# Unused memory of 64 and 128 bytes between the pools of a one-core trunk layer, so that its operands start at other places modulo 256

## The chip, the cores and the metric

The kernel runs on one core of a Trainium2 chip. The metric is the device time of one execution in microseconds (us), the median of several runs. TensorE (PE in the profile) multiplies, with a weight load (PEld) ahead of every product; VectorE is DVE, ScalarE is ACT, GpSimd is POOL; SyncE (SP) starts most of the transfers. SBUF is the memory on the chip that the engines work in: 128 partitions, and in each of them a row of bytes. When this text says where a tile starts, it is the byte within the partition.

## The reference

One layer over 512 tokens of 1024 channels, all in float32:

```
u = rmsnorm(h); proj = u @ w_in                     # conv GLU | q | k | v | r | low rank | gates A, B
c = silu(layernorm(causal_dwconv31(a * sigmoid(g)))) ; y_conv = c @ w_conv_out
o = gated linear attention(q, k, v, decay), chunks of 64, 4 heads
y_gla = (rmsnorm(o) * silu(r)) @ w_gla_out
h = h + (sigmoid(gate_a) * y_conv + sigmoid(gate_b) * y_gla) @ w_o
z = causal_dwconv3(rmsnorm(h) @ w_up)               # 2 * 2816 channels
h = h + (silu(z_a) * z_b) @ w_down ; return rmsnorm(h)
```

## The kernel before

**Three products for one.** To get float32 results from the fast float32r products, every operand is split into a high part (rounded to float32r) and a low part (the rest). `whi` and `wlo` are the parts of a tile of weights, `uh` and `ul` those of the tokens; the other pairs (`ch` and `c`, `h`, `oa`, `xq`, `usq`, `gainq`, `btmpq`, `hq`, `sumsq`, `yh` and `yl`, `ah` and `al`, `sh` and `sl`) are the same for later activations. `mm3` then issues three products, which are lines 554 to 556 of the profile, and each of them has a weight load of its own:

```
nc.tensor.matmul(acc, ll, rh, start=first, stop=False, **kw)   # 554
nc.tensor.matmul(acc, lh, rl, start=False, stop=False, **kw)   # 555
nc.tensor.matmul(acc, lh, rh, start=False, stop=last, **kw)    # 556
```

The second argument is the operand that is loaded into the array (128x128, "loaded operand" below), the third is the one that streams through it (128x512 or 128x256, "streamed operand"). In `col_tile` the weights are loaded and the activations are streamed; in `seven` (Strassen-like products with seven parts for `w_r`, `w_o` and `w_down`) and in `row_half` the activations are loaded and the weights streamed; `two_tiles` streams activations of 256 columns.

**Order.** The program is one long list of products. The list `order` says in which order the tiles of weights are needed; SyncE loads each into a `raw` tile some steps ahead, ACT makes `whi`, DVE or an adding transfer of POOL makes `wlo`. Between these, DVE runs the 31-tap convolution (line 916), which is spread in small shares over the products of the first 250 us. In time the stages are: tokens and v (to about 33 us), GLU and low rank (to 113), v, heads of the attention with q and k (to 245), out-gate r (to 284), merge (to 424), `w_o` (to 464), then up- and down-projection of the channel mixer in three groups.

**Pools.** Tiles are taken from pools, which lie in SBUF one behind the other; a pool's tiles start at fixed places. From the left: constants (`cp`), weights (`wp`: `raw`, `whi`, `wlo`, 4 of each), tokens (`up`: `u`), temporaries (`tp`: first `x` and `gain`, then small tiles, then `tmp` and `btmp`), heap (`hp`: `h`), convolution (`vp`: `c`); later the pool `ffn` takes the place of the last two. From the right end of SBUF downward, behind `edge`: the attention's tiles, later `r`, `ch`, `late` (`sums`) and `hres`. Three pieces of unused memory, `PADS = (384, 992, 768)` bytes, lie in `cp`, `edge` and `tp`. With them `raw`, `whi`, `wlo`, `u`, `x`, `gain`, `h`, `c`, the pool `ffn` and everything on the right start at multiples of 256; `tmp` and `btmp` start at 128 modulo 256.

Of the kernel before, what the change touches and what calls it, by code (L numbers as in the profile page):

```python
# [10 lines left out]
F32 = mybir.dt.float32  # L11
# [7 lines left out]
P = 128  # L19
# [35 lines left out]
WARM = (6, 1)  # L55
MID = 4
EARLY = 2
PADS = (384, 992, 768)
ET = mybir.EngineType
SEVEN = {"w_o": KT // 2, "w_down": FT // 2, "w_r": KT // 2}  # L60

# [40 lines left out]
def trunk_layer(ctx: ExitStack, tc: tile.TileContext, a: dict, out: bass.AP):  # L102
    nc = tc.nc

    def pool(name, bufs, space=None):
        kw = {"space": space} if space is not None else {}
        return ctx.enter_context(tc.tile_pool(name=name, bufs=bufs, **kw))

    def scoped(name, bufs, side="left"):
        scope = ExitStack()  # L110
        return scope, scope.enter_context(tc.tile_pool(name=name, bufs=bufs, side=side))
# [3 lines left out]
    cp = pool("const", 1)  # L115
    wp = pool("weights", 1)
    up = pool("acts", 1)
    tp = pool("temps", 1)
    ps = pool("psum", 1, bass.MemoryType.PSUM)
    dram = pool("dram", 1, bass.MemoryType.DRAM)  # L120
    edge = ctx.enter_context(tc.tile_pool(name="edge", bufs=1, side="right"))
    heap_scope, hp = scoped("heap", 26)
    conv_scope, vp = scoped("conv", 10)
# [5 lines left out]
    def nm(s):  # L129
        return f"{s}_{next(names)}"  # L130
# [27 lines left out]
        return ps.tile([P, T], F32, tag="ax", name=nm("ax"), bufs=3)  # L158


    for i, part in enumerate((cp, edge)):
        part.tile([P, PADS[i] // 4], F32, name=nm("pad"))


    eps = cp.tile([P, 1], F32, name="eps")
# [11 lines left out]
    def load_consts():  # L177
        tc.keep_in_program_order(nc.sync.dma_start(pp, a["pp"]))
        nc.gpsimd.memset(shares.bitcast(F32), -1.0 / D)
        nc.gpsimd.memset(run64, 1.0)  # L180
        nc.gpsimd.memset(run64[:, 0:T:64], 0.0)

        kf = tmp(P)
        nc.gpsimd.memset(kf, 1.0)
        nc.gpsimd.affine_select(
            kf, kf, pattern=[[1, P]], compare_op=ALU.is_ge, fill=0.0, base=0, channel_multiplier=-1
        )
        nc.gpsimd.tensor_copy(keep, kf)
        nc.gpsimd.memset(att, 0.0)
# [659 lines left out]
    prefetch(LOOK)  # L849
    v_done(3, 0, acc)  # L850
    start.__exit__(None, None, None)
    tp.tile([P, PADS[2] // 4], F32, name=nm("pad"))
    load_consts()


# [462 lines left out]
    part = [None] * KT  # L1318
# [763 lines left out]
```

## Time and profile before

| | |
|---|---|
| median of 3 runs | 813.72 us (813.64 to 814.4) |
| the profiled execution | 813.83 us, of which 812.1 us are the span from the first to the last instruction |
| PE busy | 804.1 us, 99% of the span, 4176 products |
| PEld busy | 689.3 us, 85% |
| DVE, ACT, POOL busy | 707.0 (87%), 496.1 (61%), 188.5 (23%) us |
| transfers | 116.89 MB, 144 GB/s |

A product in the trace has a start and a modelled end, and products are pipelined, so that one of 0.39 us is followed by the next after some 0.23 us. What a product costs is therefore read from the distance between two starts, called its step below, and not from its own duration. In the timeline a row begins with the start and the duration in us.

### The profile page before, as it was taken

How to read it: one execution, taken by the hardware profiler on the slowest of the kernel's cores; microseconds unless marked ns; L12 is line 12 of the kernel's file. 1: busy time of each engine (PE TensorE's matmuls, PEld its weight loads, DVE VectorE, ACT ScalarE, POOL GpSimd, SP SyncE). 2: the span in 40 equal slices, each digit the busy share in tenths (PEclk: the TensorE clock that was granted, in tenths of full speed). 3: DMA queues.
4: the chain of work that ended last, by engine and by line, in shares of the span. 5: the costliest groups of instructions: out<-in, count | busy, mean ns of one | idle time of the engine just before them, and what ended most of it. 6: DMA issues, size and time to landing. Idle time of an engine off the chain costs nothing.

```text
span 812.1 us, 11427 instructions
## 1 busy us (share of the span) xinstructions
PE 804.1 (99%) x4176; PEld 689.3 (85%) x4176; DVE 707.0 (87%) x1120; ACT 496.1 (61%) x761; POOL 188.5 (23%) x166
## 2 busy tenths in 40 slices
PE   9999999999999999999999999999999999999997
PEld 7888888788888899989888898898889988899885
DVE  6779999998998898786778899979966999789896
ACT  6667788677647785593445655456445663356555
POOL 2025434332204222022011101320123310522010
PEclk9999999999999999999999999999999999999999
DMA  8488757755832533433458523145732446334662
GB/s 333 151 196 183 187 162 174 165 134 141 216 88 89 151 122 105 153 107 102 158 135 213 171 78 105 55 153 157 152 131 80 143 117 169 104 105 171 166 129 105
DMA packets 44217, 116.89 MB, mean 144 GB/s; under 512 B 10408, under 2 KB 16048, under 8 KB 44160
## 3 DMA queue, kind: packets, MB, share of 16 engines
q1 hardware_dynamic: 36800, 90.19, 32.5%
q0 software_dynamic: 7200, 25.69, 18.3%
q8 instruction: 33, 0.54, 0.3%
q10 hardware_dynamic: 160, 0.27, 0.1%
q14 instruction: 24, 0.20, 0.1%
HBM read 110.76 MB, written 3.74 MB: 141 GB/s over the span
## 4 chain that ended last, share of the span: by engine, by line
PE 77%; DVE 15%; issue 5%; ACT 2%; POOL 1%; DVEq 0%; ACTq 0%; POOLq 0%
PE mm L554 18%; PE mm L555 18%; PE mm L556 18%; DVE c L916 5%; PE cv L555 4%; PE cv L556 4%; PE cv L554 4%; DVE aside L916 3%; PE ax L555 2%; PE ax L556 2%; PE ax L554 2%; DVE wlo L437 1%; PE mm L772 1%; ACT whi L435 1%; DVE h L1605 1%
## 5 line engine op out<-in xcount | busy, mean ns | idle before, releaser
L554 PE MATMUL mm<-uh,wlo 128*128 128x512 f32 (+1 forms) x532 | 193.8, 364 | 0.1
L555 PE MATMUL mm<-ul,whi 128*128 128x512 f32 (+1 forms) x532 | 191.5, 360 | 0.0
L556 PE MATMUL mm<-uh,whi 128*128 128x512 f32 (+1 forms) x532 | 191.4, 360 | 0.0
L437 DVE TENSOR_TENSOR wlo<-raw,whi 128x1024 fp32r<-128x1024 f32 x82 | 95.7, 1174 | 29.0 <-ACT whi L435 24.9
L405 POOL TENSOR_TENSOR raw<-raw,raw 128x512 f32<-128x512 f32 x39 | 61.2, 1569 | 240.6 <-DVE wlo L437 133.0
L554 PEld LDWEIGHTS mm<-uh,wlo 128*128 128x128 f32 x532 | 100.5, 189 | 15.4 <-DVE wlo L477 0.5
L556 PEld LDWEIGHTS mm<-uh,whi 128*128 128x128 f32 x532 | 100.4, 189 | 15.4
L555 PEld LDWEIGHTS mm<-ul,whi 128*128 128x128 f32 x532 | 100.5, 189 | 14.7
L435 ACT CAST whi<-raw 128x1024 fp32r<-128x1024 f32 x82 | 79.0, 966 | 36.7 <-PE mm L556 16.3
L468 ACT CAST whi<-raw 128x1024 fp32r<-128x1024 f32 x80 | 83.5, 1047 | 29.1 <-PE mm L556 12.8
L477 DVE TENSOR_TENSOR wlo<-raw,whi 128x1024 fp32r<-128x1024 f32 x50 | 66.1, 1328 | 7.2 <-ACT whi L468 7.0
L435 ACT CAST whi<-kept 128x1024 fp32r<-128x1024 f32 (+1 forms) x40 | 40.1, 1008 | 31.2 <-DVE kept L381 15.7
L437 DVE TENSOR_TENSOR wlo<-kept,whi 128x1024 fp32r<-128x1024 f32 (+1 forms) x40 | 47.6, 1194 | 6.2 <-ACT whi L435 6.2
L916 DVE SCALAR_TENSOR_TENSOR c<-aside,btmp,c 128x247 f32<-128x247 f32 (+13 forms) x93 | 52.3, 568 | 0.0
L916 DVE SCALAR_TENSOR_TENSOR aside<-cv,pp,aside 128x255 f32<-128x255 f32 (+6 forms) x112 | 52.0, 464 | 0.0
L916 DVE SCALAR_TENSOR_TENSOR c<-cv,pp,c 128x247 f32<-128x247 f32 (+13 forms) x93 | 43.1, 464 | 2.3 <-ACT c L912 1.4
L470 ACT ACTIVATE wlo<-raw 128x1024 fp32r<-128x1024 f32 x28 | 29.4, 1058 | 18.9 <-PE mm L554 18.9
L1793 DVE SCALAR_TENSOR_TENSOR tmp<-mm,pp,tmp 128x511 f32<-128x511 f32 (+1 forms) x42 | 31.1, 742 | 3.6 <-ACT tmp L1790 3.5
L1408 ACT COPY tmp<-mm 128x256 f32<-128x256 f32 x38 | 14.1, 370 | 30.0 <-PE mm L556 29.6
L1793 DVE SCALAR_TENSOR_TENSOR tmp<-tmp,pp,tmp 128x511 f32<-128x511 f32 (+1 forms) x32 | 27.8, 888 | 0.4
L1564 DVE TENSOR_TENSOR hres<-hres,mm 128x512 f32<-128x512 f32 (+1 forms) x37 | 24.6, 674 | 2.2 <-PE mm L556 2.1
L555 PE MATMUL cv<-ul,whi 128*128 128x512 f32 (+1 forms) x72 | 25.6, 356 | 0.0
(518 smaller groups left out, 2084.8 us busy)
## 6 DMA issues: line engine op xcount, KB each, us to landing
raw<-in_w_up_dram SPq DMA_DIRECT2D x44, 512.0 KB, 3.6
raw<-in_w_glu_dram SPq DMA_DIRECT2D x16, 512.0 KB, 5.3
raw<-in_w_down_dram SPq DMA_DIRECT2D x16, 512.0 KB, 4.1
wlo<-in_w_glu_dram POOLq DMA_DIRECT2D x12, 512.0 KB, 7.1
kept<-in_w_down_dram POOLq DMA_DIRECT2D x9, 512.0 KB, 5.5
raw<-in_w_v_dram SPq DMA_DIRECT2D x8, 512.0 KB, 6.4
raw<-in_w_qk_dram SPq DMA_DIRECT2D x8, 512.0 KB, 6.2
raw<-in_w_gb_dram SPq DMA_DIRECT2D x8, 512.0 KB, 4.5
```

What stands on the lines that cost most here:

```text
L405: work = nc.gpsimd.tensor_tensor(out, x, y, ALU.add)
L435: nc.scalar.copy(hi, raw)
L437: two_low[:] = [nc.vector.tensor_tensor(lo, raw, hi.bitcast(F32), ALU.subtract)]
L468: nc.scalar.copy(hi, raw)
L470: pace[0] = nc.scalar.mul(lo, raw, -1.0)
L477: pace[0] = nc.vector.tensor_tensor(lo, raw, hi.bitcast(F32), ALU.subtract)
L554: nc.tensor.matmul(acc, ll, rh, start=first, stop=False, **kw)
L555: nc.tensor.matmul(acc, lh, rl, start=False, stop=False, **kw)
L556: nc.tensor.matmul(acc, lh, rh, start=False, stop=last, **kw)
L916: nc.vector.scalar_tensor_tensor(out[:, j:], x[:, : half_t - j], w, out[:, j:], ALU.mult, ALU.add)
L1564: done = nc.vector.tensor_tensor(hres[t, n][:, c], hres[t, n][:, c], acc[:, c], op)
L1793: nc.vector.scalar_tensor_tensor(z[:, s:], acc[:, : T - s], w[j], z[:, s:], ALU.mult, ALU.add)
```

## The change

Three more pieces of unused memory: 64 bytes at the end of `wp`, 64 bytes at the end of `up`, 128 bytes in `vp`; and the piece in `edge` grows by 64 bytes. Nothing else is edited: the same instructions stand in the same order on every engine, with the same waits, and each tile has the same place among its pool's. What moves is where the tiles start. From the allocations of the two programs, the first byte modulo 256:

| tiles | before | after |
|---|---|---|
| `raw`, `whi`, `wlo` (`wp`) | 0 | 0 |
| `u`: `uh`, `ul` (`up`) | 0 | 64 |
| `x`, `gain`, with `kept`, `xq`, `gainq`, `oa` in their places (`tp`) | 0 | 128 |
| `tmp`, `btmp` with `btmpq` (`tp`) | 128 | 0 |
| `h`, `hq` (`hp`) | 0 | 128 |
| `c` (`vp`) | 0 | 0 |
| `ffn`: `kept`, `y`, `f`, `w`, `v`, `yh`, `yl`, `ah`, `al`, `sh`, `sl`, `usq` | 0 | 128 |
| the right side: attention, `r`, `ch`, `sums` with `sumsq`, `hres` | 0 | 192 |
| constants, with `shares` (96) and `ident` (32) | as they are | the same |

The 3929 float32r products of lines 554 to 556 and 772 have 2670 times 512 and 1259 times 256 columns. Of the streamed operand of one and the loaded operand of the next (the two that are read at the same time), the places modulo 256 differ before in 2 products of 512 columns and 65 of 256; after, in 2584 and 1156.

```
-PADS = (384, 992, 768)
+PADS = (384, 1056, 768)
+SHIFTS = (64, 64, 128)
...
-    for i, part in enumerate((cp, edge)):
-        part.tile([P, PADS[i] // 4], F32, name=nm("pad"))
+    for part, size in ((cp, PADS[0]), (edge, PADS[1]), (vp, SHIFTS[2])):
+        part.tile([P, size // 4], F32, name=nm("pad"), bufs=1)
...
-    tp.tile([P, PADS[2] // 4], F32, name=nm("pad"))
+    for part, size in ((tp, PADS[2]), (wp, SHIFTS[0]), (up, SHIFTS[1])):
+        part.tile([P, size // 4], F32, name=nm("pad"), bufs=1)
```

## The prediction

> **What bounds the kernel now.** I read the busy times first, then the waits of TensorE, then the stretches, then single starts in the timeline.
>
> ```profile
> span 812.1 us, 11427 instructions
> PE 804.1 (99%) x4176; PEld 689.3 (85%) x4176; DVE 707.0 (87%) x1120; ACT 496.1 (61%) x761; POOL 188.5 (23%) x166
> PEclk9999999999999999999999999999999999999999
> ...
> PE mm L675 <- DVE ones L647: 1.1, 1, 1.1
> PE cv L554 <- DVE r L1621: 0.3, 1, 0.3
> ...
> PEld ax L1251 <- DVE state L1240: 1.1, 3, 0.5
> PEld mm L555 <- DVE wlo L437: 0.7, 2, 0.5
> ```
>
> TensorE is busy all the time at the full granted clock, and the last four rows, among the longest waits of the products and of their weight loads for another engine, add up to 3 us. So the span is the sum of the steps of 4176 products, and only what changes a step, or makes TensorE wait where it does not now, changes the time. The steps of two quiet stretches (first and last rows of runs of products of one kind):
>
> ```profile
> 341.99 0.28 PE L555 MATMUL cv<-sumsq,whi 128*128 128x256 f32 x1
> ...
> 342.95 0.40 PE L554 MATMUL mm<-oa,wlo 128*128 128x512 f32 x1
> 343.19 0.40 PE L555 MATMUL mm<-oa,whi 128*128 128x512 f32 x1
> 343.42 0.39 PE L556 MATMUL mm<-oa,whi 128*128 128x512 f32 x1
> ...
> 344.11 0.39 PE L556 MATMUL mm<-oa,whi 128*128 128x512 f32 x1
> ...
> 791.70 0.39 PE L555 MATMUL mm<-wlo,sh 128*128 128x512 f32 x1
> ...
> 800.31 0.39 PE L554 MATMUL mm<-whi,al 128*128 128x512 f32 x1
> ```
>
> Eight products of 256 columns take 0.96 us, 120.0 ns each; 38 of 512 columns take 8.61 us, 226.6 ns each. The difference, 106.6 ns, pays for 256 columns; so 512 columns cost 213.2 ns, and in both cases 13.4 ns are left over that do not depend on the columns. That remainder comes once for each product and its weight load, and it is the only thing of TensorE's that the change can touch: 13.4 ns x 3929 float32r products are 52.6 us, 6.5% of the span. In between, after the switch from 256 to 512 columns at 342.95, five products take 1.16 us, 232 ns each, before the steps fall back to 226.6: the remainder is not a constant of the array, it depends on what stood before.
>
> **What of it hangs on the place.** In these stretches all operands start at 0 modulo 256. Two kinds of products do not. In the first, `btmpq` is streamed from 128 between `usq` and weights at 0:
>
> ```profile
> 532.89 0.28 PE L554 MATMUL cv<-btmpq,wlo 128*128 128x256 f32 x1
> 533.00 0.28 PE L555 MATMUL cv<-usq,whi 128*128 128x256 f32 x1
> 533.12 0.28 PE L556 MATMUL cv<-btmpq,whi 128*128 128x256 f32 x1
> ...
> 534.30 0.28 PE L554 MATMUL ax<-gainq,wlo 128*128 128x256 f32 x1
> 534.41 0.28 PE L555 MATMUL ax<-xq,whi 128*128 128x256 f32 x1
> ```
>
> Twelve products take 1.41 us, 117.5 ns each, where 12 at 0 take 1.44. With both rows rounded to 0.01 us this is 2.5 ns less, give or take 0.8; I take 2. The first two show steps of 0.11 and 0.12 us, the one at 534.30 again 0.11. So the place does move the step, and here downward. In the second, `sum` is streamed from 128, against `shares` at 96 and then weights at 0, in two products of 512 columns:
>
> ```profile
> 306.65 0.39 PE L556 MATMUL mm<-h,whi 128*128 128x512 f32 x1
> 306.88 0.63 PE L1028 MATMUL ax<-sum,shares 128*128 128x512 f32 x2
> 307.34 0.28 PE L554 MATMUL mm<-uh,wlo 128*128 128x256 f32 x1
> ...
> 331.26 0.62 PE L1028 MATMUL ax<-sum,shares 128*128 128x512 f32 x2
> 331.72 0.39 PE L554 MATMUL mm<-oa,wlo 128*128 128x512 f32 x1
> ```
>
> Both pairs take 0.46 us, 230 ns each: 3.4 ns more than the quiet 226.6, though 2 to 4 ns less than the 232 to 234 at which the first products after a switch from 256 columns run (0.47 us for the two from 342.95), which the second pair is. One row says faster, one row says either; neither shows a long run with a constant distance, and that is what the change makes.
>
> **The change part by part.** Nothing is added, removed or moved in time on any engine or queue: no instruction, no wait, no transfer. Four kinds of users see other places.
>
> Products. 1156 of 256 columns now have the streamed and the next loaded operand apart, 65 had before: 1091 more. At the -2 ns of the `btmpq` row this is -2.2 us. Of 512 columns 2584 are apart, 2 before. Their price is bounded by -11.4 ns below (the remainder shrinks to 2, see the rivals) and by +5.4 above (every step is 232, as after a switch). I take -2 ns, since the remainder was the same 13.4 ns for both widths and so belongs to the weight load and not to the columns, and the `btmpq` row, the only one with more than two products in a row, prices such a load: -5.2 us.
>
> The elementwise engines. They read the tiles at other places too, and these rows say that it costs nothing (`tmp` and `btmp` start at 128, `f`, `ah` and `raw` at 0):
>
> ```profile
> L1807 DVE TENSOR_TENSOR f<-tmp,tmp 128x512 f32<-128x512 f32 x11 | 7.5, 683 | 0.2
> L1813 DVE TENSOR_TENSOR al<-f,ah 128x512 fp32r<-128x512 f32 x11 | 7.5, 683 | 0.4 <-ACT ah L1812 0.4
> L435 ACT CAST whi<-raw 128x512 fp32r<-128x512 f32 x16 | 9.9, 620 | 0.6 <-POOL raw L405 0.6
> L1066 ACT CAST ch<-btmp 128x512 fp32r<-128x512 f32 x8 | 4.7, 616 | 0.1
> ```
>
> DVE's 683 ns from 128 and from 0 are equal, ACT's 616 and 620 nearly; I put 0 for both.
>
> The transfers. `raw` and `wlo`, most of the bytes, stay at 0; `x`, `gain`, `kept`, `hres`, `rx` and the stored `y` go from 0 to 128 or 192, `tmp` from 128 to 0. The one pair of rows of equal size:
>
> ```profile
> out_dram<-tmp SPq DMA_DIRECT2D x2, 256.0 KB, 2.2
> out_dram<-hres SPq DMA_DIRECT2D x2, 256.0 KB, 2.1
> ```
>
> From 128 it took 0.1 us longer than from 0. The loads are covered by TensorE, which waits for none of them above; uncovered are the first `x` at the start and the last store at the end, so +0.1 to +0.2 us, which is rounding.
>
> The cover. A shorter step is worth its length only where the weights are ready, and that is DVE's and ACT's matter:
>
> ```profile
> 100.00:180.00 80.00, 79.87 (x361) 65.89 (x360) 79.87 (x172) 63.13 (x105) 30.54 (x28) 1.00 0.64 155
> 180.00:245.00 65.00, 64.97 (x297) 54.10 (x297) 61.91 (x136) 39.46 (x76) 10.97 (x11) 1.00 0.64 155
> 530.00:680.00 150.00, 150.00 (x841) 131.53 (x840) 128.21 (x169) 79.88 (x111) 33.66 (x26) 1.00 0.46 130
> ```
>
> (The columns are PE, PEld, DVE, ACT, POOL busy with counts.) From 100 to 180 us DVE, with the convolution, has 0.13 us of idle time; 361 products x 2 ns = 0.7 us would be gained there, and 0.6 of it is lost to waiting for DVE. From 180 to 245 DVE has 3.1 us free against 0.6, from 530 to 680 21.8 against 1.7: nothing is lost.
>
> Sum: -2.2 - 5.2 + 0.6 = -6.8 us. The profiled execution took 813.83 us (span 812.1 and 1.7 around it), 0.1 above the median of 813.72. 813.8 - 6.8 = 807.0 us.
>
> **A rule against it.** The Trainium skill, "TensorE: Matmul & The Clock Gate", section "Step-by-step: what each phase is for", says that TensorE reads the streamed operand and the weights through two independent ports, so that loading the next weights takes no bandwidth from the running product; "SBUF — State Buffer", section "Who interferes with whom", says that TensorE and ScalarE never wait on anyone. By these the place could not matter and the time would stay at 813.8. The trace disagrees in part: its remainder is 13.4 ns, and 117.5 ns stand against 120.0 with nothing else changed.
>
> **The rivals.**
>
> *The two reads stop hindering each other (much faster).* If the remainder is mostly two streams that meet at the same place modulo 256 all the time, a constant distance ends it. What is then left shows in the plain float32 products, which run each product in two records:
>
> ```profile
> 183.88 0.59 PE L1253 MATMUL ax<-state,q 128*128 128x256 f32 x2
> 184.31 0.59 PE L1251 MATMUL ax<-h,att 128*128 128x256 f32 x2
> ```
>
> 0.43 us for two records, 215 ns each, about as long as 512 columns (213.2): a remainder of 2. Then 11.4 ns x (1091 + 2584) = 41.9 us go, less 4.0 of the 4.1 us from 100 to 180 and 0.3 of 3.4 from 180 to 245, where DVE holds: about 776; half of that gives 794. Against it: the `btmpq` products had a distance of 128, and their steps do not fall to 109. Chance 0.15.
>
> *No distance matters, only a break in the run (no change).* In the `btmpq` rows the place alternates from product to product, 128, 0, 128. It may be the alternation that shortens steps, while any constant distance settles at 226.6 and 120.0 again. After the change the streamed operand starts at the same place as the one before it in about 9 of 10 products, so little is left: a tenth of 7.4 us, within 0.2% (1.6 us, about what a measurement of this kernel tells from no change). 813.1. The rule above gives the same. Chance 0.15.
>
> *The quiet step is the good case (slower).* 226.6 is near the low end of the steps of 512 columns seen (the 230 and 232 above), 120.0 the high end of those of 256. Where the distance keeps the two reads from settling, the wide products go to 230 to 232 and the narrow ones to 118: 2584 x 3.4 to 5.4 ns = +8.8 to +14.0, less 2.2: 820 to 825.5, with nothing to hide it, as TensorE is the bound everywhere. It decides as soon as a wide product loses 0.85 ns, for that eats the 2.2 us. For it: the pairs at line 1028. Against it: the second pair is quicker than the products that otherwise stand there. Chance 0.28.
>
> **How the numbers follow.** The forecast (a remainder smaller by 1 to 5 ns) has the other 0.42: 807.0, from 811.6, if the narrow products alone gain, to 798, if the wide ones gain twice what I took. With the much faster case, faster by over 0.2% is 0.57; same 0.15; slower 0.28. The range reaches into both outer cases: down to 790, past half of the large gain, which leaves out about 0.10, and up to 824, which leaves out the upper end of the slow case, about 0.06.
>
> **What would show it.** The starts in the timeline, in a long run of one kind: streamed tokens at 64 against weights at 0 (up-projection, from 500 us), loaded `sh`, `ah`, `yh` at 128 against streamed weights at 0 (the last 60 us). 224 to 225 and 117 to 119 ns there bear out the forecast, 226.6 and 120.0 the rival of no change, 228 and more the slow one, 216 the large gain. The durations at lines 435, 1807 and 1813 should stay at 620 and 683, the store of `tmp` and `hres` at 2.1 to 2.2 us. The sum is wrong if the steps differ with the distance, 64, 128 and 192 not being alike (I have a row for 128 alone), or if from 100 to 245 us DVE becomes what TensorE waits for although the steps got shorter.

## The result, and the profile after

The change made the kernel slower: 820.52 us, median of 4 runs (819.18 to 821.69), against 813.88 for the kernel before beside it. The ratio is 1.0081, with a 95% interval from 1.0069 to 1.0094. In a later series of 5 runs it was 820.03 us, ratio 1.0073 [1.0059, 1.0087]. The forecast was 807.0 and faster; the time lies inside the range and is that of the rival "the quiet step is the good case".

The busy times of the profiled execution (821.69 us):

```profile
span 819.9 us, 11427 instructions
PE 812.4 (99%) x4176; PEld 688.5 (84%) x4176; DVE 708.1 (86%) x1120; ACT 496.5 (61%) x761; POOL 190.1 (23%) x166
PEclk9999999999999999999999999999999999999999
```

The span grew by 7.8 us, PE's busy time by 8.3, and nothing else grew by more than 1.6. The clock is the same. The waits of products and weight loads for another engine:

```profile
PE mm L676 <- DVE ones L648: 1.1, 1, 1.1
PE cv L555 <- DVE r L1623: 0.2, 1, 0.2
...
PEld ax L1253 <- DVE state L1242: 0.5, 2, 0.2
...
PEld mm L556 <- DVE wlo L438: 0.3, 1, 0.3
```

They are no longer than before. So the 7.8 us are in the steps. These are the starts at the places of the program that the prediction quoted (lines 554 to 556 of before are 555 to 557 here):

```profile
39.64 0.40 PE L557 MATMUL mm<-uh,whi 128*128 128x512 f32 x1
...
74.88 0.40 PE L555 MATMUL mm<-uh,wlo 128*128 128x512 f32 x1
...
344.73 0.28 PE L555 MATMUL cv<-sumsq,wlo 128*128 128x256 f32 x1
...
346.11 0.40 PE L555 MATMUL mm<-oa,wlo 128*128 128x512 f32 x1
...
348.91 0.28 PE L555 MATMUL mm<-uh,wlo 128*128 128x256 f32 x1
...
499.83 0.39 PE L557 MATMUL cv<-uh,whi 128*128 128x512 f32 x1
...
519.98 0.39 PE L555 MATMUL mm<-uh,wlo 128*128 128x512 f32 x1
...
798.82 0.40 PE L555 MATMUL mm<-whi,sl 128*128 128x512 f32 x1
...
809.79 0.39 PE L557 MATMUL mm<-whi,ah 128*128 128x512 f32 x1
```

- Tokens at 64 against weights at 0, wide: 151 steps from 39.64 take 35.24 us, 233.4 ns each. The same kind of product from 499.83: 88 steps in 20.15 us, 229.0 ns. The same distance gives two values; more on that below.
- `sumsq` at 192, narrow: 12 steps in 1.38 us, 115 ns, 120.0 before.
- `oa` at 128, wide: 12 steps in 2.80 us, 233.3 ns. Before, these fell back to 226.6 after five products; now they don't.
- Loaded `sh`, `yh`, `ah` at 128, streamed weights at 0: 47 steps in 10.97 us, 233.4 ns; 226.6 before.

All starts of both traces, summed: the 512-column products took 620.3 us before and 630.8 after, those of 256 columns 167.6 and 165.0. That is +10.5 and -2.6, together +7.9, which is the growth of the span. The 3929 products that the prediction priced have +10.2 and -1.9 of this; the 32 and 80 products on other lines have +0.3 and -0.8, with what they wait.

The stretch with `btmpq`, where `usq` now starts at 128 and `btmpq` at 0, so that the place still alternates:

```profile
537.92 0.28 PE L555 MATMUL cv<-btmpq,wlo 128*128 128x256 f32 x1
...
539.33 0.28 PE L555 MATMUL ax<-gainq,wlo 128*128 128x256 f32 x1
```

Twelve products in 1.41 us, exactly as before. The elementwise groups, the stores and the three stretches:

```profile
L436 ACT CAST whi<-raw 128x512 fp32r<-128x512 f32 x16 | 9.9, 620 | 0.5 <-POOL raw L406 0.4
L1809 DVE TENSOR_TENSOR f<-tmp,tmp 128x512 f32<-128x512 f32 x11 | 7.5, 682 | 0.2
L1815 DVE TENSOR_TENSOR al<-f,ah 128x512 fp32r<-128x512 f32 x11 | 7.5, 681 | 0.3 <-ACT ah L1814 0.3
L1068 ACT CAST ch<-btmp 128x512 fp32r<-128x512 f32 x8 | 4.7, 616 | 0.1
```

```profile
out_dram<-tmp SPq DMA_DIRECT2D x2, 256.0 KB, 2.6
out_dram<-hres SPq DMA_DIRECT2D x2, 256.0 KB, 2.5
```

```profile
100.00:180.00 80.00, 80.00 (x360) 65.70 (x359) 78.81 (x170) 64.47 (x107) 30.53 (x27) 1.00 0.64 156
180.00:245.00 65.00, 65.00 (x296) 54.12 (x295) 61.90 (x138) 40.24 (x77) 11.11 (x12) 1.00 0.64 152
530.00:680.00 150.00, 150.00 (x843) 130.48 (x842) 125.88 (x168) 78.98 (x111) 33.51 (x25) 1.00 0.47 132
```

682 and 681 against 683, 620 and 616 as before: the elementwise engines don't notice. From 100 to 180 us DVE now has 1.2 us of idle time where it had 0.13, as longer products on TensorE would give it.

### The profile page after: what moved, and what is told of

Its sections match the earlier page's. It is cut to its first block, busy times and chain, and to the rows that moved or that the text cites. A ratio compares the mean times of both kernels' runs of the same rounds, so it can differ in the third digit from the quotient of the medians.

```text
span 819.9 us, 11427 instructions
## 1 busy us (share of the span) xinstructions
PE 812.4 (99%) x4176; PEld 688.5 (84%) x4176; DVE 708.1 (86%) x1120; ACT 496.5 (61%) x761; POOL 190.1 (23%) x166
## 4 chain that ended last, share of the span: by engine, by line
PE 97%; DVE 1%; ACT 1%; issue 0%; DVEq 0%; ACTq 0%
PE mm L555 23%; PE mm L556 23%; PE mm L557 23%; PE cv L555 4%; PE cv L557 4%; PE cv L556 4%; PE ax L555 3%; PE ax L556 3%; PE ax L557 3%; PE mm L773 2%; PE ax L1253 1%; PE cv L773 1%; PE ax L1255 1%; PE ax L1235 1%; PE ax L684 1%; PE mm L780 0%
## 5 line engine op out<-in xcount | busy, mean ns | idle before, releaser
L555 PE MATMUL cv<-uh,wlo 128*128 128x512 f32 (+1 forms) x72 | 25.6, 355 | 0.0
```

## The experiments

Theory A in the texts below says that a product's step hangs on the distance, modulo 256, between the place of its streamed operand and that of the next loaded one. The other theories are told in the texts themselves, and what became of each stands behind its text. "Distance" below is streamed minus loaded.

### The steps by themselves

A separate kernel without the layer: 50 sections of 36 float32r products each, nothing beside them, so that nothing but the places and the columns differs from section to section. It leaves out the whole layer and computes only these products.

```
def section(n, count, cols, streams, loads):
    for i in range(count):
        m = streams[i % len(streams)] // 4 + T * (i % 4)   # first word of the streamed operand
        w = loads[i % len(loads)] // 4 + P * (i % 8)       # of the loaded one
        nc.tensor.matmul(acc, loaded[:, w : w + P], streamed[:, m : m + cols], ...)
```

> Not the layer: 50 sections of 36 float32r products each, with nothing beside them, so that only the steps of TensorE are measured. The loaded and the streamed operand start at chosen places modulo 256. Theory A (the distance of the two operands sets the step, whatever else the core does): the sections at distance 0 run at 226.7 ns (512 columns) and 120.0 ns (256), whether both operands stand at 0 or both at 64, 128 or 192; the sections at 64, 128 and 192 run at 229 to 234 ns and 116 to 119 ns, as in the changed layer. Theory B (a start that is no multiple of 256 is what costs): both at 64 runs as slowly as 64 against 0, above 229 ns. Theory C (the step comes from what ACT, DVE and transfers do at the same time): here all sections are alike, at one step for each width.

The timeline of single sections ("wide" has 512 columns, "narrow" 256; wide at distance 0, 32, 64, 128 and 192; narrow at 0, 64 and 192; wide with both operands at 64; wide at 4; and three sections with alternating places, told below). A row puts together 32 to 35 products: the start, then the time from the first start to the last end.

```profile
19.50 7.87 PE L109 MATMUL bank<-streamed,loaded 128*128 128x512 f32 x34
36.01 8.09 PE L109 MATMUL bank<-streamed,loaded 128*128 128x512 f32 x34
52.80 7.95 PE L109 MATMUL bank<-streamed,loaded 128*128 128x512 f32 x34
86.09 8.06 PE L109 MATMUL bank<-streamed,loaded 128*128 128x512 f32 x34
119.68 8.09 PE L109 MATMUL bank<-streamed,loaded 128*128 128x512 f32 x34
161.27 4.12 PE L109 MATMUL bank<-streamed,loaded 128*128 128x256 f32 x33
178.32 4.05 PE L109 MATMUL bank<-streamed,loaded 128*128 128x256 f32 x33
212.34 3.90 PE L109 MATMUL bank<-streamed,loaded 128*128 128x256 f32 x33
229.19 7.89 PE L109 MATMUL bank<-streamed,loaded 128*128 128x512 f32 x34
278.81 8.20 PE L109 MATMUL bank<-streamed,loaded 128*128 128x512 f32 x34
295.48 8.21 PE L109 MATMUL bank<-streamed,loaded 128*128 128x512 f32 x35
303.75 8.15 PE L109 MATMUL bank<-streamed,loaded 128*128 128x512 f32 x35
312.09 3.90 PE L109 MATMUL bank<-streamed,loaded 128*128 128x256 f32 x32
```

Of 7.87 us, 0.39 are the last product's own; the other 7.48 are 33 steps of 226.7 ns. In the same way 8.09 gives 233, 7.95 gives 229, 8.06 gives 232, 8.20 gives 237. The settled steps, as means of the last 24 of each section:

| distance | 0 | 16 | 32 | 48 | 64 | 80 | 96 | 112 | 128 | 144 | 160 | 176 | 192 | 208 | 224 | 240 |
|---|---|---|---|---|---|---|---|---|---|---|---|---|---|---|---|---|
| wide, ns | 226.7 | 231.7 | 233.3 | 233.3 | 228.9 | 231.1 | 233.3 | 231.1 | 232.1 | 233.3 | 234.4 | 233.3 | 233.3 | 234.7 | 233.3 | 226.7 |
| narrow, ns | 120.0 | 118.6 | 116.7 | 118.3 | 117.8 | 120.0 | 120.0 | 113.3 | 118.8 | 118.7 | 117.3 | 119.4 | 113.3 | 119.2 | 118.3 | 117.1 |

At 4 bytes a wide product takes 236.7 ns, the most of all, at 8 bytes 233.3. Both operands at 64, at 128 or at 192 give 226.67, as at 0. Only the loaded one at 64 gives 233.3, as the streamed one at 192 does; only the loaded one at 192 gives 228.9, as the streamed one at 64 does. So it is the difference that counts, and nothing but these products is needed for it: no other engine is at work here, and no transfer of operands. At distance 0 the two widths go opposite ways: of 16 distances, it is the best for wide products, together with 240, and the worst for narrow ones, together with 80 and 96. B and C fall.

Theory A holds as long as the places stay the same from product to product. Four sections let both places alternate between 0 and 128. Where each streamed operand has the place of the next loaded one (distance 0 throughout, as theory A counts it), the steps are 230.0 ns wide (the row at 295.48) and 116.7 narrow (312.09), and not 226.7 and 120.0. Where it has the place of its own product's loaded operand, so that the next one lies 128 away, they are 228.3 (303.75) and 116.7, and not 232.1 and 118.8. So the distance to the next loaded operand does not set the step alone. Whether its own loaded operand counts as well, or the change of place itself, these sections leave open; at constant places the two loaded operands stand alike.

### Everything at 64

The kernel before, with all operands of the products moved together by 64 bytes, so that every distance stays what it was.

```
-PADS = (384, 992, 768)
+PADS = (448, 928, 768)
```

> The kernel before with 64 bytes more in the first piece and 64 less in the one at the right edge: all tiles that stood at 0 modulo 256 stand at 64, tmp and btmp at 192, and the distances are those of before. Theory A (distance): steps of 226.7 and 120.0 ns and 813 to 815 us. Theory B (multiples of 256): steps of 230 to 233 and 118 ns in most products and 819 to 822 us, as with the change.

813.87 us against 813.89, ratio 0.9998 [0.9988, 1.0007]. The sums are 620.4 us for 512 columns and 167.6 for 256, as before. That is theory A's forecast (813 to 815 us) and not B's (819 to 822): in the layer, too, a common step of 64 bytes costs nothing.

### The tokens alone

Of the change, only the step of `u` to 64 is made (the piece in `up` brings the pools behind it back to their places).

```
-SHIFTS = (64, 64, 128)
+SHIFTS = (64, 192, 0)
```

> One part of the change alone: the tokens' pool at 64, everything else at the places of before. 1320 wide and 612 narrow products stream tokens or later sums from there against weights at 0, 312 wide ones load them. Theory A: the products that touch the pool run as after the change (230.4 and 118.1 ns streamed, 233.3 loaded), all others at 226.7 and 120.0: 1320 x 3.7 + 312 x 6.6 - 612 x 1.9 ns = +5.8 us, 819 to 820.5 us. If what costs is instead that places alternate between pools (a rival, since the change made four places of one), the tokens alone, all at one place in long runs, cost under 2 us: 813.5 to 816 us.

815.20 us, ratio 1.0019 [1.0009, 1.0029]: a small loss where a large one was expected. The long run of wide tokens:

```profile
39.66 0.39 PE L555 MATMUL mm<-uh,wlo 128*128 128x512 f32 x1
...
74.91 0.39 PE L556 MATMUL mm<-ul,whi 128*128 128x512 f32 x1
```

154 steps in 35.25 us: 228.9 ns, the value of the separate kernel for 64, and not the 233.4 of the changed layer. The 512-column sum is 624.6 us (+4.3), the 256-column sum 164.8 (-2.8): the 583 narrow products with tokens at 64 took 116.8 ns on average, and the 300 wide ones that load from this pool at 64 took 233.3, as their distance of 192 says. Theory A's forecast was missed: it priced the streamed tokens by the changed layer, at +3.7 ns wide and -1.9 narrow, where they moved by +1.9 and -3.3. The time lies in the band of the rival, but not for its reason: products at a constant distance did become dearer, from 226.9 to 233.3 ns where the pool is loaded.

### Entry, width and type

A second separate kernel, again without the layer, of 69 sections in three parts. The first runs a section at distance 64 behind sections of other kinds. The second replaces one operand by a single word that is read again and again, or both by bf16. The third puts runs of 12 or 24 narrow products between runs of 12 or 24 wide ones at 0; here it is the loaded operand's place that is set to 64, 144 and 224, which makes the distances 192, 112 and 32.

```
x, y = s[:, m : m + cols], l[:, w : w + P]
if kind == "one word streamed":
    x = s[:, m : m + 1].to_broadcast([P, cols])
if kind == "one word loaded":
    y = l[:, w : w + 1].to_broadcast([P, P])
nc.tensor.matmul(acc, y, x, ...)
```

> Not the layer: sections of products alone, as in e1. Three questions. (1) In the changed layer the long run of the tokens' products at distance 64 goes 233, 233, 234 ns, with the tokens alone moved it goes 226, 229, 232: same operands, same distance. Theory A1 (a distance has more than one cycle to settle in, and what stood before decides): the sections at 64, entered from wide ones at 0, 128 and 32 and from narrow ones, settle on at least two different means. Theory A2 (something else in the layer): all settle at 228.9, as in e1. (2) Theory A (two reads at a time): with one word streamed again and again, or one word loaded, the remainder over 213.3 ns falls well below 13 and the distance no longer matters; if the remainder belongs to the weight swap alone, it stays at 13.4 ns. With bf16 operands, half the bytes, the remainder falls too, to a few ns. (3) Runs of 12 narrow at distance 0, 64, 144, 224 between 12 wide at 0: with 64 or 144 as the place of the streamed operand I expect no better than e1's single runs, 118 ns in the mean.

Rows of single sections: narrow at 0 behind wide at 64; narrow at 64 behind wide at 64; one word streamed, wide; bf16, wide; bf16, narrow.

```profile
51.71 4.12 PE L118 MATMUL bank<-streamed,loaded 128*128 128x256 f32 x33
...
64.26 3.90 PE L118 MATMUL bank<-streamed,loaded 128*128 128x256 f32 x33
...
129.97 7.50 PE L118 MATMUL bank<-streamed,loaded 128*128 128x512 f32 x34
...
170.31 7.50 PE L118 MATMUL bank<-half,turned 128*128 128x512 bf16 x34
...
201.40 3.77 PE L118 MATMUL bank<-half,turned 128*128 128x256 bf16 x33
```

- Entry. Wide products at 64 settled at 228.9 behind each of five predecessors (wide at 0, 32 and 128, narrow at 0 and at 64); 233.3 was not reached in this way, as theory A2 says. Narrow products at 64 did show two cycles: 113.3 ns here (3.90 us less 0.28 for the last, over 32 steps), 117.8 in the first kernel, where narrow ones stood before, and 117.8 again in a run of five in this kernel, which stood behind wide ones at 64 as the 113.3 did. So the kind of product that stood before does not decide alone.
- Type. In bf16 a wide product takes 215.83 ns and a narrow one 109.17, at 0, 64, 128 and 192 alike. Their difference, 106.66 ns, is the price of 256 columns; 2.5 ns remain. This is the 215.7 ns that the Trainium skill ("TensorE: Matmul & The Clock Gate", "Wait — 56ns, not 53.3ns?") gives for 512 columns, 512/2.4 + 2.5: for bf16 the rows agree with it, for float32r they show 226.67 to 236.7.
- Which read. With one word streamed, float32r falls to 215.83 ns at distance 0 and 64, and to 111.67 for narrow products at 0. With one word loaded, wide products do not fall, against the expectation: they take 231.1 ns at distance 0 (226.7 with the whole operand) and 231.7 at 64 (228.9). Narrow ones at 0 fall from 120.0 to 113.3. For wide products, what lies above 2.5 ns therefore needs the float32r stream through many addresses; the loaded operand need not come from many. How the two reads hinder each other no run shows, and no section leaves the weight load out.
- Short runs. Twelve narrow products took 119.4 ns each at distance 0, 117.75 at 192, 118.7 at 112, 116.5 at 32. The 113.3 of long runs at 112 and 192 is not reached. Nor is it in runs of 24, which hold 117.8 at 192 from the first step on and 119.3 at 112, so the length alone is not what keeps them from it. Twelve wide ones behind a switch took 228.8 to 229.8 on average, with steps such as 233 236 228 233 231 226 before they settled.

### Narrow products at 192, and at 32

The first kernel's table asks for another arrangement: wide products stay at distance 0, and only the weights that meet the 256-column tokens move. The `whi` and `wlo` slots get 64 more words, and the weights of `two` start 16 words into them, which makes the distance 192; with 56 words it is 32.

```
+ROOM, APART = 64, 16        # the second kernel: 64, 56
-                hi = wp.tile([P, D], F32R, tag="whi", name=nm("whi"), bufs=4)[:, :n]
+                at = APART if name == "two" else 0
+                hi = wp.tile([P, D + ROOM], F32R, tag="whi", name=nm("whi"), bufs=4)[:, at : at + n]
...
-PADS = (384, 992, 768)
+PADS = (128, 224, 0)
```

> The kernel before (all places at 0), with the weights of the 256-column units alone moved: their whi and wlo begin 64 bytes into the slot, so that the streamed operand lies 192 above the loaded one. Each of the eight slots is 256 bytes larger, and the unused pieces shrink to (128, 224, 0). Theory A: e1 gives 113.3 ns at distance 192 against 120.0 at 0; some 1190 narrow products gain up to 6.7 ns, -8 us, of which runs of 12 to 24 between wide ones keep half to all: 806 to 810 us, wide products unchanged at 226.7. If no gain survives in short runs (rival): 812 to 814.

> As the kernel with the narrow products' loaded weights 64 bytes further, but 224 bytes further, so that streamed minus loaded is 32 modulo 256. Theory A, with the steps measured in runs of 12 between wide products (116.5 at 32 against 117.8 at 192 and 119.4 at 0, and wide products behind them 0.7 ns dearer): narrow sum down by about 2.9 x 1100 = 3.2 us, wide sum up by up to 0.7 x 300 = 0.2: 810.7 to 811.2, against 812.1 at 192. Rival (short runs never reach their settled cycle in the layer, so all distances of narrow products but 0 give about the same): 811.9 to 812.5.

| | time, us | ratio to before | 512 columns, us | 256 columns, us |
|---|---|---|---|---|
| before | 813.94 and 813.97 beside the two | | 620.3 | 167.6 |
| narrow at 192 | 812.07 (811.63 to 812.82) | 0.9979 [0.997, 0.9988] | 620.5 | 165.4 |
| narrow at 32 | 812.00 (811.4 to 813.09) | 0.9976 [0.9967, 0.9985] | 620.9 | 165.1 |

Both beat the kernel before, and so the changed one too, by a small margin. The size that theory A gave from long runs was missed. In the kernel at 192:

```profile
284.67 0.28 PE L557 MATMUL mm<-ul,whi 128*128 128x256 f32 x1
...
285.24 0.28 PE L556 MATMUL mm<-uh,wlo 128*128 128x256 f32 x1
...
339.61 0.28 PE L556 MATMUL mm<-sumsq,wlo 128*128 128x256 f32 x1
...
342.44 0.40 PE L556 MATMUL mm<-oa,wlo 128*128 128x512 f32 x1
```

Behind a pause, five steps take 0.57 us, 114 ns each, but 24 steps behind wide products take 2.83 us, 118 ns. Over the layer the mean of the 1259 narrow products falls from 119.8 ns to 118.0 at 192 and 117.7 at 32. Between these two the distance matters little, as the rival in the second text says; that it isn't 0 is worth about 2 ns. At distance 64 the 583 narrow products of the tokens took 116.8 ns with the tokens alone moved and 118.1 in the changed layer. Distance 240, which in the first separate kernel costs wide products nothing and has 117.1 ns for narrow ones, was not tried in the layer.

### All but the tokens

The rest of the change, with `u` left at 0.

```
-SHIFTS = (64, 64, 128)
+SHIFTS = (0, 128, 128)
```

> The rest of the change, with the tokens' pool back at 0. If the parts add up, what the whole costs and the tokens alone do not: 820.5 - 815.2 = 5.3 us, so 819 to 819.5. If the parts influence each other through the cycles that products settle in (theory A1), the long run of the tokens' products is back at 226.7 (in the change it ran at 233.3, alone at 229.0) and the sum does not hold: 816 to 818.

818.16 us, ratio 1.0050 [1.0035, 1.0065], between the two forecasts. The wide tokens, whose distance is 0 again, are back:

```profile
39.62 0.39 PE L556 MATMUL mm<-ul,whi 128*128 128x512 f32 x1
...
74.97 0.39 PE L556 MATMUL mm<-ul,whi 128*128 128x512 f32 x1
```

156 steps in 35.35 us, 226.6 ns. Means of the steps by place, in the layer:

| products (count) | before | tokens alone | all but tokens | changed |
|---|---|---|---|---|
| wide, `u` streamed from 64, loaded 0 (1275) | 227.6 | 229.5 | 227.6 | 230.4 |
| wide, weights streamed from 0, loaded 128 (567) | 227.1 | 227.2 | 232.5 | 233.2 |
| wide, weights streamed from 0, loaded 64 (300) | 226.9 | 233.3 | 227.4 | 233.3 |
| wide, streamed from 128, loaded 0 (182) | 228.0 | 228.2 | 232.7 | 232.5 |
| wide, streamed from 192 and 0 in turn, loaded 0 (128) | 228.2 | 228.4 | 236.0 | 235.2 |
| narrow, `u` streamed from 64, loaded 0 (583) | 120.1 | 116.8 | 120.1 | 118.1 |
| narrow, streamed from 128, loaded 0 (327) | 119.7 | 119.8 | 119.4 | 119.2 |
| narrow, streamed from 192, loaded 0 (75) | 120.1 | 120.0 | 115.6 | 115.8 |

(The places and counts are those of the changed kernel; wide steps that hold a wait are left out. Where another kernel leaves these operands at 0, the row gives the same products there. The third row has, besides the tokens, those `sums` that lie in the tokens' pool, at 64 and not at 192.) The two parts cost 1.3 and 4.2 us by their medians, together 5.5; the whole change cost 6.6. By the spans of the profiled executions, from which the table is made, they cost 1.4 and 4.4 and the whole 7.8. Of the missing 2 us there, 1.1 lie in the first row, where the tokens run at 230.4 in the whole change and at 229.5 alone, and 0.8 in the sixth, with 118.1 against 116.8. The fifth row shows again that the distance is not all. Its products come in threes, streamed from 192, 0 and 192, and the row has the first two, which a product with another place follows. They take 235 to 236 ns, more than either distance has by itself (233.3 and 226.7); the third, which another at 192 follows, takes 230. Their loaded operands all start at 0, so the change of the streamed place counts here.

### The changed kernel again

Nothing is edited; the question is whether the 233.3 of the tokens' long run belongs to the program or to the execution.

> The changed kernel itself, unedited, with more runs and another profile. In its first profile the tokens' long run (streamed 64, loaded 0, from 33 to 136 us) went at 233.3 ns a product; with the same two places it went at 229.0 in the kernel with the tokens alone at 64 and in the separate kernel of long runs. Theory D (one distance has two settled cycles, and which one an execution falls into is settled by small shifts in time at the start): the run times fall into two groups, near 819.4 and near 821.6, with few between; where the profiled execution is one of the low group, its long run goes at 229.0 ns. Rival (the cycle is fixed by what the program has at the other places, 128 and 192): the long run goes at 233.3 in every profile, also where the total is near 819.4, and the 2 us between the groups lie elsewhere.

> The same kernel, a third profiled execution. Theory D: 229.0 ns in the long run if the total is near 819.4, 233.3 if it is near 821.6. Rival: 233.3 in both cases.

The stretch from 40 to 75 us (columns: PE, PEld, DVE, ACT, POOL busy with counts, then the granted clock, the share of the DMA engines and GB/s), in the first profile, the second and the third of the same kernel:

```profile
40.00:75.00 35.00, 35.00 (x152) 28.35 (x151) 28.75 (x64) 25.58 (x41) 12.46 (x12) 1.00 0.80 181
```

```profile
40.00:75.00 35.00, 35.00 (x155) 28.71 (x154) 29.14 (x66) 26.04 (x43) 12.52 (x13) 1.00 0.81 186
```

```profile
40.00:75.00 35.00, 35.00 (x151) 28.35 (x151) 29.27 (x66) 25.58 (x43) 11.96 (x13) 1.00 0.80 180
```

152 and 151 products fit in the first and third, 155 in the second: by the starts, 233.3, 228.9 and 233.3 ns a product. So the same instructions at the same places settle in one cycle in one execution and in another in the next; the rival, that the program's other places fix it, is refuted. A later stretch of the same kind, in the first profile and then in the second, has it the other way round:

```profile
139.05 0.39 PE L556 MATMUL mm<-ul,whi 128*128 128x512 f32 x1
...
141.79 0.39 PE L556 MATMUL mm<-ul,whi 128*128 128x512 f32 x1
```

```profile
139.23 0.40 PE L556 MATMUL mm<-ul,whi 128*128 128x512 f32 x1
...
141.79 0.40 PE L555 MATMUL mm<-uh,wlo 128*128 128x512 f32 x1
```

12 steps in 2.74 us (228.3 ns) against 11 in 2.56 (232.7): with ends rounded to 0.01 us, these are the same two cycles. Each stretch falls into its cycle for itself. The other half of theory D, that the times fall into two groups, isn't borne out: ten runs lie at 819.2, 819.3, 819.6, 819.7, 820.0, 820.1, 820.4, 820.5, 821.5 and 821.7. That several stretches choose apart would give such a spread, but only three profiles show the choices. What decides them was not found; the second and third executions ran on one chip, so it is not a difference between chips.

## Why the prediction was wrong

- **The bound** was read rightly. The span changed by what the steps changed, +7.9 against +7.8 us, and the waits stayed under 3 us.
- **The narrow products** were right in their sum: -2.2 us forecast, -1.9 measured. That is in part luck. They were not alike, as the text feared: -2.0 ns at 64, -0.5 at 128, -4.3 at 192. And the `btmpq` row was no price for a constant distance: its places alternate, it takes 1.41 us after the change as before, and in the first separate kernel narrow products at alternating places take 116.7 ns, where a constant 128 has 118.8.
- **The wide products** are the step that failed: "I take -2 ns, since the remainder was the same 13.4 ns for both widths and so belongs to the weight load and not to the columns". For each of the 2584 the step grew by 3.9 ns on average, so that the term is +10.2 us in place of -5.2. The reason was wrong on both counts. The remainder of a wide product is not the weight load's alone: it falls to 2.5 ns when the stream comes from one word, and does not fall when the load does. And of the 16 distances, it is equal for the two widths at 0 alone: with 106.66 ns for 256 columns, the first separate kernel has 13.3 ns there at 512, 384, 320 and 256 columns, though 16.7 at 480 (a step of 216.67 ns) and 16.0 at 448 (202.67); at distance 64 it is 15.6 for wide products and 11.1 for narrow ones. A row of narrow products thus said nothing of wide ones.
- **The rows that did speak of wide products** were in the text: the pairs at line 1028, 230 ns each, and the five products at 232 after a switch. They were read as two products and a transient, and left to the rival. They were the only rows with wide products off the quiet cycle, and both lay above it, though two steps between starts rounded to 0.01 us are good to some 5 ns only.
- **The cover, the elementwise engines** cost nothing, as said. The 0.6 us set down as lost to DVE fell away with the gain that it belonged to.
- **The stores** were forecast at 2.1 to 2.2 us and were 2.6 and 2.5 in the first profile, 2.3 and 2.2 in the second, 2.4 and 2.3 in the third. They move together from one execution to the next, so the place is not shown to be the cause; none is more than 0.4 us longer than before.
- **The rivals.** The slow one, with a chance of 0.28, came true in its place and its size: 230 to 232 for wide products (measured means by place from 230.4 to 235.2), 118 for narrow ones, 820 to 825.5 us. Its mechanism fits in part: the reads do settle, but in cycles with a longer mean step. Of the much faster case, 216 ns is reached only where float32r gives way to bf16 or the stream comes from one word; no distance tried ends the remainder. The case of no change was half right: alternating places do shorten narrow steps (116.7 ns). But a constant distance does not settle at 226.6, with 240 as the one exception. With this case fell, for float32r, what the prediction drew from the rule of the Trainium skill ("TensorE: Matmul & The Clock Gate", "Step-by-step: what each phase is for") that the weight load takes no bandwidth from the running product: only the loaded operand's place was moved to 64 in the first separate kernel, and the step went from 226.7 to 233.3 ns. In bf16 the rows agree with the rule.
- **What would make it wrong** was named rightly: 64, 128 and 192 are not alike, and 64 and 192 differ by 4.4 ns for the same two operands with their parts exchanged.

## What to carry to other kernels

Where a core does nothing but float32r products, each with a weight load of its own, let all operands of the 512-column products, streamed and loaded, start at the same place modulo 256, and read this from steps, since no wait and no share of busy time shows it; for 256 columns the distances 32, 64 and 192 were worth 2 to 4 ns against 0. A price read on one width is not a price for another: the sign can turn, and where one short row of the right kind stands against a long row of the wrong kind, believe the right kind. A difference of 1 us between two executions can be one of several cycles into which the same instructions settle, so take two profiles before explaining it by the edit.

## What the runs showed of the hardware

- While the places stay the same from product to product, the step of a float32r product hangs on streamed minus loaded place modulo 256: 226.7 ns (0 and 240) to 236.7 (4 bytes) with 512 columns, 113.3 (112 and 192) to 120.0 (0, 80, 96) with 256. Where they alternate between 0 and 128, it is 228.3 or 230.0 and 116.7, which the distance alone does not give. Bf16 shows 215.8 and 109.2 at each of the places tried.
- Settled steps repeat in short cycles, such as 226 229 232 at distance 64, and one distance can have two of them (228.9 and 233.3 for wide products in the layer, 113.3 and 117.8 for narrow ones). A cycle can hold for over a hundred products, and the same program can be in another one at the same place in its next execution.
- After a change of width, some five steps of wide products (233 236 228 233 231) and two of narrow ones (114 119) differ from the settled ones even at distance 0. In a program that switches every 12 products, that is 228.9 ns for a wide product and 119.4 for a narrow one, where long runs have 226.7 and 120.0.
- No constant distance among the 18 tried (the 16 of the table, 4 and 8 bytes) took a wide product below 226.67 ns.
